# One hybrid attention layer on one core: the kernel lists the steps of TensorE, ScalarE and VectorE itself, adds Strassen products up in PSUM, and keeps high and low parts in one tile

## Chip, cores and metric

The kernel runs on one core of one Trainium2 chip. The metric is the device time of one execution in microseconds (us), lower is better. The core's engines are TensorE (PE, matmuls; its weight loads are shown apart as PEld), VectorE (DVE), ScalarE (ACT), GpSimd (POOL) and SyncE (SP, which here only issues transfers). Matmuls write into PSUM banks of 128 x 512 float32; everything else lies in SBUF tiles with 128 partitions.

## The reference, cut to what matters

One layer, batch 1, 512 tokens, model width 2048, three branches of four heads with 128 columns each.

```
hn   = rmsnorm(x, norm_g)                       # 512 x 2048
proj = hn @ w_in                                # 2048 x (6144 + 4 + 6144)
# the first 6144 columns: q, k, v and a gate path for branches A, B, C
# then 4 forget-gate logits, then 3 x 2048 merge-gate logits
ya = forgetting_attention(rms(q), rms(k), v, f_logit)      # A: softmax, causal
yb = chunked_relpos_attention(rms(q), rms(k), v, rel_bias) # B: softmax, 576-key band
yc = stick_breaking_attention(q, k, v)                     # C: products of 1 - sigmoid
ys = stack(ya, yb, yc) * silu(gate paths)
up = ys[n] @ w_up[n]                            # for each branch: 512 x 512 by 512 x 2048
merged = sum_n sigmoid(gate_n + b_gate) * up_n
out = x + merged @ w_out                        # 2048 x 2048
```

All inputs and outputs are float32.

## The kernel before

**Numbers and tiles.** Everything is kept transposed: model columns on partitions, the 512 tokens along a row. A product of float32 is made of three matmuls in the type fp32r: each operand is split into a high part (a copy rounded to fp32r) and a low part (the rest), and `mm3` (L115 to L118) adds up high x high, high x low and low x high. For a split, ScalarE writes the high part and VectorE the low part:

```python
def split_to(hi, lo, src):                              # L93
    nc.scalar.activation(hi, src, AF.Copy)              # L94
    nc.vector.tensor_sub(lo, src, f(hi))                # L95
```

In the program's names `wh` and `wl` are the parts of a weight piece, `x1h`, `x1l`, `x2h`, `x2l` those of the two halves of the normalized input (eight tiles of 128 x 512 each), `yh`, `yl` those of a branch's output, `m1`, `m2` those of the merged result. `split_off` (L104, so L106 and L107 in the profile) does the same with the low part put off by some splits.

**Units.** The program is a list of units; a unit has one weight piece of eight 128 x 128 blocks (128 x 1024; in the up-projections six blocks, 128 x 768), its load, its split, its matmuls, and what follows them. The stages in order:

- 0 to 64 us: the first head of branch C with its q, k, v and gate columns together (`first_quad`, L652), while x arrives and its norm is worked out.
- up to 117 us: four columns of merge gates, straight (`col_task`, L320, 512 columns of tokens a matmul).
- up to about 1100 us: the rest of the input projection in pairs of columns by a Strassen–Winograd scheme (`pair_task`, L334): two columns by two halves of the tokens in seven products P1 to P7 of 24 matmuls of 256 columns, in place of eight. Products 1, 2, 3 and 5 take x1 and x2; P6, P7 take `t23`, P4 takes `t`, sums of them made once in `combos` (L282). The weights' sums are made on VectorE for each pair (L351 to L363). A head uses two pairs (q and k, then v and gate) with pairs of merge gates between; their attention work lies beside later pairs. Merge gates go to HBM (`gl`), branch outputs too (`yd`).
- up to about 1235 us: the up-projections (`up_units`, L778): two units for each of 16 tiles of the model width, 12 tiles of y in each tile's sum; sigmoid (L806) on the gates that come back from HBM, products and sums on VectorE (L808 to L811), then the sums for the last Strassen stage (`merged_combos`, L826).
- to the end: the output projection, eight pairs, each with the residual added (L877 on).

**Banks and sums of a pair.** Each of the seven products takes the next of four PSUM banks `acc`, and its result is taken out by itself. A regular pair runs its products in the order 1, 2, 6, 7, 4, 5, 3; `u`, `c1` and `c2` are SBUF tiles, and one ScalarE copy and seven VectorE sums (L383 to L404) put the two columns together. The first pair, and the first of the output projection, run in the order 1, 2, 5, 3, 6, 7, 4 (`late=True`), in which what P6, P7 and P4 need may come later.

**What sets the order.** PE runs its instructions in the order in which the loop over the units (L962 on) writes them. Attention steps are hung on units by the table `OFF`. ScalarE and VectorE are in written order only up to unit 16 (`OFF["bgn"]`); from there on the framework's scheduler picks their order by its own model. A unit's split is written two units ahead (`LA`), its load five more (`LD`). Buffers: 21 tiles of 128 x 512 (`t2`), 56 for x, t, y and m parts, six for loaded weights.

## Time and profile before

| | before |
|---|---|
| median of 3 runs | 1401.34 us (1400.13 to 1402.62) |
| profiled execution | 1402.7 us, its span 1401.0 us |
| loads of w_in, w_up and w_out | 192 x 512, 32 x 384, 32 x 512 KB; 3.6, 3.1 and 3.8 us from issue to landing |
| moved by DMA | 180.57 MB, 129 GB/s over the span |
| share of 16 DMA engines, main queue | 39.3% |
| VectorE, splits of 128 x 1024 weights (L95) | 364 in 445.1 us |
| ScalarE, the same splits (L94) | 364 in 385.8 us |

The span is the time from the first to the last instruction of the profiled execution; the 1.7 us around it belong to its time. Busy time is the time in which an engine worked on something; waiting isn't in it. Matmuls overlap in the array, so a matmul's own duration (about 0.28 us for 256 columns) is longer than the distance from one start to the next. "Granted clock" is the share of TensorE's full clock that it was given. In rows of single instructions the columns are start (us), duration (us), engine, line, operation, output <- inputs, shape; x2 or more at the end is a group of such instructions, and a bracket tells how long the engine had waited and for whom.

### The profile page before, as it was taken

To read this page: it belongs to the slowest core of one execution; us is meant where nothing else is said; L and a number is where in the kernel's file an instruction comes from. 1 tells how busy PE (TensorE), PEld (TensorE's weight loads), DVE (VectorE), ACT (ScalarE), POOL (GpSimd) and SP (SyncE) were. 2 spreads that over 40 slices of the span, in tenths; PEclk is the share of its full clock that TensorE was granted. 3 is DMA by queue.
4 is the path that set the end of the run, shared out by engine and by line. 5 is a ranking of instruction groups with operands and counts; after the bars stand their busy time and mean duration, and the time that the engine had idled before them with its cause. 6 is when DMAs were issued, how large, how long until landed. Compare 5 with 4: busy or idle time off the path is not lost.

```text
span 1401.0 us, 25194 instructions
## 1 busy us (share of the span) xinstructions
PE 1370.5 (98%) x10306; PEld 1315.3 (94%) x10306; DVE 1163.9 (83%) x1687; ACT 743.9 (53%) x1095; POOL 4.3 (0%) x21
## 2 busy tenths in 40 slices
PE   7999999999999999999999999999999799999999
PEld 5778899999999999999999999999999688889999
DVE  4898898988879888898888878878888588898886
ACT  6655555544555555455556545555456655453332
POOL 0000000000000000000000000000000000000000
PEclk9999999999999999999999999999999899999999
DMA  9333233243333433333333333333335466535542
GB/s 338 129 107 101 90 95 115 99 128 106 100 123 111 128 104 120 124 102 125 116 112 121 95 126 119 99 121 93 128 104 174 164 202 206 170 95 172 166 148 80
DMA packets 68468, 180.57 MB, mean 129 GB/s; under 512 B 7656, under 2 KB 13672, under 8 KB 68352
## 3 DMA queue, kind: packets, MB, share of 16 engines
q1 hardware_dynamic: 64896, 174.69, 39.3%
q10 hardware_dynamic: 3456, 4.26, 0.9%
q8 instruction: 81, 1.33, 0.4%
q14 instruction: 35, 0.29, 0.1%
HBM read 159.24 MB, written 19.69 MB: 128 GB/s over the span
## 4 chain that ended last, share of the span: by engine, by line
PE 93%; DVE 3%; ACT 2%; DMA 1%; issue 1%; SPq 0%; ACTq 0%; DVEq 0%
PE acc L116 27%; PE acc L118 27%; PE acc L117 27%; PE att L117 3%; PE att L116 3%; PE att L118 3%; PE att L577 1%; DMA sg<-gl 1%; DVE wl L95 1%; PE att L546 1%; PE att L599 1%; PE att L431 1%; PE att L600 0%; PE att L598 0%; DMA x<-in_xT 0%
## 5 line engine op out<-in xcount | busy, mean ns | idle before, releaser
L94 ACT ACTIVATE wh<-raw 128x1024 fp32r<-128x1024 f32 x364 | 385.8, 1060 | 507.2 <-PE acc L117 455.4
L95 DVE TENSOR_TENSOR wl<-raw,wh 128x1024 fp32r<-128x1024 f32 x364 | 445.1, 1223 | 90.0 <-ACT wh L94 89.2
L116 PE MATMUL acc<-x1h,wh 128*128 128x256 f32 (+1 forms) x752 | 221.9, 295 | 12.9 <-ACT wh L106 9.6
L117 PE MATMUL acc<-x1l,wh 128*128 128x256 f32 (+1 forms) x752 | 219.3, 292 | 2.1 <-DVE x1l L107 2.1
L116 PE MATMUL acc<-x2h,wh 128*128 128x256 f32 (+1 forms) x752 | 220.9, 294 | 0.0
L118 PE MATMUL acc<-x1h,wl 128*128 128x256 f32 (+1 forms) x752 | 219.4, 292 | 1.1 <-DVE wl L107 1.0
L118 PE MATMUL acc<-x2h,wl 128*128 128x256 f32 (+1 forms) x752 | 218.5, 291 | 0.0
L117 PE MATMUL acc<-x2l,wh 128*128 128x256 f32 (+1 forms) x752 | 218.4, 290 | 0.0
L116 PE MATMUL acc<-t23h,wh 128*128 128x256 f32 x704 | 200.6, 285 | 0.0
L118 PE MATMUL acc<-t23h,wl 128*128 128x256 f32 x704 | 199.2, 283 | 0.0
L117 PE MATMUL acc<-t23l,wh 128*128 128x256 f32 x704 | 199.1, 283 | 0.0
L116 PEld LDWEIGHTS acc<-x1h,wh 128*128 128x128 f32 x752 | 144.9, 193 | 16.4 <-ACT wh L106 9.6
L117 PEld LDWEIGHTS acc<-x1l,wh 128*128 128x128 f32 x752 | 144.9, 193 | 4.9 <-DVE x1l L107 2.5
L118 PEld LDWEIGHTS acc<-x1h,wl 128*128 128x128 f32 x752 | 144.9, 193 | 4.2 <-DVE wl L107 2.3
L116 PEld LDWEIGHTS acc<-x2h,wh 128*128 128x128 f32 x752 | 144.8, 193 | 3.0 <-issue 0.2
L117 PEld LDWEIGHTS acc<-x2l,wh 128*128 128x128 f32 x752 | 144.7, 192 | 2.3 <-issue 0.2
L118 PEld LDWEIGHTS acc<-x2h,wl 128*128 128x128 f32 x752 | 144.5, 192 | 2.3 <-DVE wl L107 0.4
L117 PEld LDWEIGHTS acc<-t23l,wh 128*128 128x128 f32 x704 | 135.0, 192 | 0.0
L116 PEld LDWEIGHTS acc<-t23h,wh 128*128 128x128 f32 x704 | 135.0, 192 | 0.0
L118 PEld LDWEIGHTS acc<-t23h,wl 128*128 128x128 f32 x704 | 134.9, 192 | 0.0
L116 PE MATMUL acc<-t,wh 128*128 128x256 f32 x352 | 100.4, 285 | 0.0
L117 PE MATMUL acc<-t,wh 128*128 128x256 f32 x352 | 99.5, 283 | 0.0
(277 smaller groups left out, 2834.9 us busy)
## 6 DMA issues: line engine op xcount, KB each, us to landing
raw<-in_w_col SPq DMA_DIRECT2D x192, 512.0 KB, 3.6
raw<-in_w_out SPq DMA_DIRECT2D x32, 512.0 KB, 3.8
gl<-c SPq DMA_DIRECT2D x48, 256.0 KB, 2.0
raw<-in_w_up SPq DMA_DIRECT2D x32, 384.0 KB, 3.1
sg<-gl SPq DMA_DIRECT2D x48, 256.0 KB, 4.6
x<-in_xT SPq DMA_DIRECT2D x16, 256.0 KB, 6.2
xn<-in_xn SPq DMA_DIRECT2D x16, 256.0 KB, 6.2
xr<-in_xT SPq DMA_DIRECT2D x16, 256.0 KB, 4.8
```

Source lines behind the costliest of these rows:

```text
L94: nc.scalar.activation(hi, src, AF.Copy)
L95: nc.vector.tensor_sub(lo, src, f(hi))
L116: nc.tensor.matmul(ps, lh, rh, start=start, stop=False)
L117: nc.tensor.matmul(ps, lh, rl, start=False, stop=False)
L118: nc.tensor.matmul(ps, ll, rh, start=False, stop=stop)
L431: nc.tensor.matmul(first_ps[:2 * NH, :], w2[:, kt, :], xs[kt][j], start=kt + j == 0, stop=kt + j == KT)
L546: nc.tensor.transpose(ps[:, blk(i)], st["p"][i][:, blk(j)], identf)
L577: nc.tensor.matmul(ps[:, i * P:], nu_r if i == j else nones_r, part, start=i == j and part is st["lk"][j][0], stop=False)
L599: nc.tensor.matmul(o, vl[:, blk(j)], st["h"][j], start=False, stop=False)
```

## The change

The change has three parts.

**1. The order is made by the kernel.** All of PE, ScalarE and VectorE is now under `manual_schedule`, so that these three engines run what the program writes, in the order in which it writes it. Each step (a split, a softmax stage, the matmuls of one k-tile) is a generator that yields what it waits for (an `Event`, a number of `Slots` of a pool) and then `(engine, cost, due)` ahead of each instruction. `Flow.run` keeps a clock for each engine and always writes next the step that could start first, and of several the one that is due first. Costs are formulas, not measured times.

```diff
+class Flow:
+    LATE = (0.3, 0.12, 0.12)
...
+    def run(self):
+        while self.tasks:
...
+                    key = (max(self.clock[t.engine], t.ready), t.due)
+                    if best is None or key < best[0]:
+                        best = key, t
...
+            self.clock[e] = start + t.cost
+            t.ready = self.clock[e]
+            self.fin = t.fin = self.clock[e] + self.LATE[e]
...
+def mm_us(n, x=1):
+    return x * max(0.115, n / 2400 + 0.0133)
...
+def act_us(n, x=1):
+    return x * (0.075 + 0.00095 * n)
...
+def dve_us(n, x=1):
+    return x * (0.1 + 0.00105 * n)
...
-    ctx.enter_context(tc.manual_schedule(engines={mybir.EngineType.PE}))
-    begin = ExitStack()
-    begin.enter_context(tc.manual_schedule(engines={mybir.EngineType.Activation, mybir.EngineType.DVE}))
+    ctx.enter_context(tc.manual_schedule(engines={mybir.EngineType.PE, mybir.EngineType.Activation,
+                                                  mybir.EngineType.DVE}))
...
-OFF = dict(cs=4, ct=12, nk=5, nq=4, s=12, t=18, v=3, av=10, nrm=7, xg=10, bgn=16, fb=30, a0=16, b0=23, last=3)
+KEPT = 1
+NX = 28
+NR = 6
+
+OFF = dict(cs=3, ct=12, s=11, t=17, v=1, av=8, s1=8, t1=13, v1=0, av1=3, fb=30, a0=17, b0=27)
```

**2. Products of a pair add up in PSUM.** In a regular pair the order is now 1, 2, 6, 5, 7, 3, 4. P6 goes on in the bank of P1, P7 in that of P6, P4 in that of P7 (`onto`), P3 in that of P5; P2 has a bank of its own. The pool `acc` is now three: two banks of the first kind and one each of the others. ScalarE copies the sum so far out of a bank after P1, P6 and P5 (and after P4 where no residual is to be added), and VectorE adds after P2, P7 and P3. The matmuls are the same ones; the signs of some sums (`t4`, w6, w7) are turned for it. The first pair and the first output pair are as before in this, in the order 1, 5, 2, 3, 6, 7, 4. The last output pair is like the others now: the residual is added at P3, P7 and P4.

```diff
-        order = (1, 2, 5, 3, 6, 7, 4) if late else (1, 2, 6, 7, 4, 5, 3)
+            self.order = (1, 5, 2, 3, 6, 7, 4) if late else (1, 2, 6, 5, 7, 3, 4)
...
+            bank = (0, 1, 2, 0, 0, 1, 2)[i] if self.late else {2: 1, 5: 2, 3: 2}.get(p, 0)
+            onto = None if self.late else {6: 1, 7: 6, 4: 7, 3: 5}.get(p)
+            more = onto is not None
...
+                if more:
+                    yield self.ev[onto]
+                    self.ps[p] = self.ps[onto]
...
-                elif p == 7:
-                    add(u[:, RH], u[:, LH], ps)
...
-                elif p == 5:
-                    add(c2[:, RH], u[:, RH], ps)
-                    add(u[:, LH], u[:, LH], ps)
...
+                    if p == 6:
+                        yield a
+                        nc.scalar.activation(self.u[:, RH], ps, AF.Copy)
+                    elif p == 7:
+                        yield ev[5]
+                        yield v
+                        add(self.c2[:, RH], self.c2[:, RH], ps)
+                        finished("c2r", self.c2[:, RH])
```

**3. High and low parts lie in one tile.** `Parts` is a tile of 128 x 2 x 2 x 256: for each half of the tokens the high part, then the low part. A matmul over all 512 tokens reads its moving operand through `two(...)`, two runs of 256 with 256 others between. 28 such tiles stand for the 56 of before.

```diff
-    def xt(s):
-        return xp.tile([P, S], F32R, tag="x", name=nm(s))
...
+            self.t = xp.tile([P, 2, 2, HS], F32R, tag="x", name=nm(s))
+            self.hi, self.lo = self.t[:, :, 0, :], self.t[:, :, 1, :]
```

**Around the up-projections.** The sigmoid of a gate may be written only after the SiLU of the last head. A split of y is written four to one units ahead of the first up-projection. Of the sums for the last stage, those that need only the first half of the merged result (`merged_a`: m1) are made as soon as it is there; `merged_b` makes m2, then the differences, and, once the last up-projection's matmuls are written (`up_done`), the splits of m23 and m4 with due times of 7 and 14 us after it.

```diff
+            yield last_head.event("g")
+            yield ACT, act_us(S) + 0.1
+            nc.scalar.activation(g, g, AF.Sigmoid, bias=bg[:, n * DT + d:n * DT + d + 1])
...
+        yield up_done
+        yield xps, 1
+        due = up_done.t + 0.3 * k
+        ev = Event()
+        m23[k] = Parts("m23", [ev, ev])
+        yield from split(m23[k].hi, m23[k].lo, two(t), S, ev, (due + 7.0,))
```

**What stands in the rows of the engines.** ScalarE at the start of the up-projections, before (`y_13144` is the last head's SiLU, `sg` a merge gate, `yh` the high part of a branch's output, `wh` that of an up-projection's weights):

```order
L604 ACT_TABLE_LOAD
L604 ACTIVATE y_13144<-y_13144 128x512
L94 ACTIVATE yh_13053<-yr_13051 128x512
L605 ACT_TABLE_LOAD
L605 ACTIVATE y_13144<-y_13144 128x512
L106 ACTIVATE wh_13160<-raw_12955 128x768
L94 ACTIVATE yh_13095<-yr_13093 128x512
L806 ACT_TABLE_LOAD
L806 ACTIVATE sg_13099<-sg_13099,small_in 128x512
L607 ACT_TABLE_LOAD
L607 ACTIVATE y_13144<-y_13144 128x512
L806 ACT_TABLE_LOAD
```

The same place now (the split of y is a row of L239, with both halves in one instruction):

```order
L239 ACTIVATE y_12733<-yr_12664 128x2x256
L239 ACTIVATE y_12774<-yr_12666 128x2x256
L239 ACTIVATE y_12771<-y_12516 128x2x256
L239 ACTIVATE y_12718<-yr_12716 128x2x256
L239 ACTIVATE wh_12813<-raw_12556 128x768
L239 ACTIVATE y_12721<-yr_12719 128x2x256
L239 ACTIVATE y_12724<-yr_12722 128x2x256
L1316 ACT_TABLE_LOAD
L1316 ACTIVATE sg_12725<-sg_12725,small_in 128x512
L709 ACTIVATE c_12715<-acc_12519 128x256
L239 ACTIVATE wh_12849<-raw_12605 128x768
L239 ACTIVATE y_12767<-yr_12765 128x2x256
```

The steps of the last SiLU (L604 to L607) are no longer here but earlier, and the sigmoids begin after one table load.

VectorE at the start of the output projection, before (`m` the merged result, `m2l` and `m1l` the low parts of its last tile, `m23l` those of the sums for P6 and P7, `mt` and `mu` the sums themselves, `wl` a weight's low part):

```order
L811 TENSOR_TENSOR m_2349_14277<-m_2349_14277,sg_2330_14163 128x512
L830 TENSOR_TENSOR mt_2352_14290<-m_2349_14277,m_2340_14216 128x256
L831 TENSOR_TENSOR m_2340_14216<-m_2340_14216 128x256
L95 TENSOR_TENSOR m2l_2351_14287<-m_2349_14277,m2h_2350_14286 128x512
L832 TENSOR_TENSOR mt_2352_14290<-m_2349_14277,m_2340_14216 128x256
L95 TENSOR_TENSOR m1l_2354_14296<-m_2340_14216,m1h_2353_14295 128x512
L833 TENSOR_TENSOR mu_2327_14154<-mt_2352_14290,m_2349_14277 128x256
L95 TENSOR_TENSOR m23l_2356_14300<-mt_2230_13713,m23h_2355_14299 128x512
```

The same place now, from behind the last sum of the merged result (its tile is `sg_2068`) and one weight split; L625 is a sum of weights:

```order
L241 TENSOR_TENSOR m1_2096_13975<-sg_2056_13750,m1_2096_13975 128x2x256
L625 TENSOR_TENSOR raw_2073_13838<-raw_2073_13838,raw_2053_13732 128x1024
L241 TENSOR_TENSOR m23_2100_13982<-mt_1913_13017,m23_2100_13982 128x2x256
L241 TENSOR_TENSOR m23_2101_13983<-mt_1941_13160,m23_2101_13983 128x2x256
L241 TENSOR_TENSOR m23_2102_13984<-mt_1968_13301,m23_2102_13984 128x2x256
L241 TENSOR_TENSOR m23_2103_13985<-mt_1996_13443,m23_2103_13985 128x2x256
L241 TENSOR_TENSOR m23_2104_13986<-mt_2023_13584,m23_2104_13986 128x2x256
L241 TENSOR_TENSOR wl_2113_14035<-raw_2073_13838,wh_2112_14034 128x1024
L241 TENSOR_TENSOR m23_2105_13987<-mt_2051_13726,m23_2105_13987 128x2x256
L241 TENSOR_TENSOR m23_2106_13988<-mt_2078_13866,m23_2106_13988 128x2x256
L241 TENSOR_TENSOR wl_2119_14073<-raw_2053_13732,wh_2118_14072 128x1024
L241 TENSOR_TENSOR m2_2108_14023<-sg_2068_13818,m2_2108_14023 128x2x256
```

The last m1 now needs nothing of the last sum; the last m2, its split once directly behind the sum of the merged result, now stands behind seven of the eight m23 splits.

VectorE in the second regular pair (at 150 us of the profile before), before: `c_224` in the last row is the sum after that pair's P2, by which P2's bank comes free; `lk`, `lkl`, `z` belong to the first head's attention, L351 to L361 are sums of weights.

```order
L95 TENSOR_TENSOR lkl_1140<-lk_1329,lkh_1137 128x384
L351 TENSOR_TENSOR raw_1529<-raw_1393,raw_1395 128x1024
L565 SCALAR_TENSOR_TENSOR lk_1375<-z_1133,lk_1375 128x512
L95 TENSOR_TENSOR wl_1496<-raw_1105,wh_1495 128x1024
L360 TENSOR_TENSOR raw_1393<-raw_1391,raw_1393 128x1024
L566 TENSOR_TENSOR lk_1375<-lk_1375,m_104 128x128
L95 TENSOR_TENSOR wl_1526<-raw_1391,wh_1525 128x1024
L95 TENSOR_TENSOR lkl_1139<-lk_1375,lkh_1136 128x512
L385 TENSOR_TENSOR c_224_1367<-u_1366,acc_1399 128x256
```

The same pair now: L679 is the sum after P2, L1019 to L1026 are attention steps.

```order
L241 TENSOR_TENSOR wl_1329<-raw_1144,wh_1328 128x1024
L679 TENSOR_TENSOR c_1370<-c_1327,acc_1330 128x256
L1025 SCALAR_TENSOR_TENSOR lk_1262<-z_1169,lk_1262 128x384
L1026 TENSOR_TENSOR lk_1262<-lk_1262,m_104 128x128
L241 TENSOR_TENSOR lkl_1351<-lk_1220,lkh_1350 128x256
L241 TENSOR_TENSOR wl_1372<-raw_983,wh_1371 128x1024
L1025 SCALAR_TENSOR_TENSOR lk_1307<-z_1298,lk_1307 128x512
L1026 TENSOR_TENSOR lk_1307<-lk_1307,m_104 128x128
L241 TENSOR_TENSOR lkl_1260<-lk_1262,lkh_1259 128x384
L241 TENSOR_TENSOR wl_1408<-raw_1114,wh_1407 128x1024
```

The sum after P2 now stands ahead of the attention steps, which are spread between the weight splits; and its bank `acc_1330` is P2's alone, asked for again by the next pair.

## The prediction

> **What bounds it now.** I read the page first, then busy time by stage, then TensorE's own waits.

> ```profile
> span 1401.0 us, 25194 instructions
> PE 1370.5 (98%) x10306; PEld 1315.3 (94%) x10306; DVE 1163.9 (83%) x1687; ACT 743.9 (53%) x1095; POOL 4.3 (0%) x21
> ...
> PE 93%; DVE 3%; ACT 2%; DMA 1%; issue 1%; SPq 0%; ACTq 0%; DVEq 0%
> ```

> TensorE (PE) is busy for 98% of the span and holds 93% of the chain that ended last. A busy PE is not always a PE at full pace, so the next view, busy time by stage, is read with its column PEclk (after the POOL column).

> ```profile
> 65.00:122.00 57.00, 53.90 (x268) 45.49 (x267) 52.69 (x111) 28.81 (x54) 0.00 (x0) 0.99 0.32 99
> 150.00:160.00 10.00, 6.68 (x42) 6.42 (x40) 7.65 (x13) 3.12 (x4) 0.00 (x0) 0.83 0.19 54
> 160.00:1080.00 920.00, 920.00 (x7565) 913.70 (x7564) 782.87 (x1093) 500.77 (x727) 1.51 (x3) 1.00 0.36 113
> 1080.00:1112.00 32.00, 24.12 (x123) 19.63 (x122) 18.73 (x32) 24.92 (x35) 0.00 (x0) 0.84 0.60 213
> 1112.00:1232.00 120.00, 120.00 (x534) 99.48 (x533) 97.99 (x150) 61.25 (x86) 0.00 (x0) 1.00 0.54 177
> 1232.00:1242.00 10.00, 6.69 (x44) 6.29 (x43) 9.93 (x17) 6.54 (x14) 0.00 (x0) 0.83 0.21 57
> ```

> From 160 to 1080 us PE is busy for 920.00 of 920.00 us at full clock, from 1112 to 1232 for 120.00 of 120.00. Nothing can be won there. The time above PE's own work lies in four places: 65 to 122 (norm, and first Strassen pair), 150 to 160 (second regular pair), 1080 to 1112 (start of the up-projections), 1232 to 1242 (start of the output projection). PE's waits by releaser give the sizes; the columns after the colon are us in total, times, longest.

> ```profile
> PE acc L116 <- ACT wh L106: 9.6, 1, 9.6
> PE att L116 <- ACT yh L94: 7.1, 2, 5.3
> PE acc L116 <- DVE c L385: 3.3, 1, 3.3
> PE acc L116 <- ACT m1h L94: 2.8, 1, 2.8
> PE acc L117 <- DVE x1l L107: 2.1, 2, 1.5
> PE acc L118 <- DVE wl L107: 1.0, 1, 1.0
> PE att L117 <- DVE yl L95: 0.8, 2, 0.6
> PE acc L117 <- DVE m1l L95: 0.5, 1, 0.5
> ```

> The 9.6 us are the first load and split. The other 17.6 us have a second price, which the clock column shows after three of the waits and at the up-projections:

> ```profile
> 121.00:124.40 3.40, 3.40 (x16) 3.40 (x17) 1.71 (x2) 1.33 (x2) 0.00 (x0) 0.51 0.37 136
> 1101.00:1111.00 10.00, 5.63 (x13) 4.19 (x14) 4.84 (x7) 6.96 (x10) 0.00 (x0) 0.51 0.03 10
> ```

> After the two L117 waits the granted clock is 0.51 for 3.4 us: half of that, 1.7 us, is lost. In the ten microseconds to 1111 PE ran 5.63 us at 0.51: 2.8 us lost. The stage rows 150 to 160 and 1232 to 1242, at 0.83 over 10 us, give 1.7 us each. So PE's removable loss is 17.6 + 1.7 + 2.8 + 1.7 + 1.7 = 25.5 us of 1401.0.

> **PE's own work.** The order of instructions has the same matmuls before and now: 8836 of 256 columns, 1077 of 512, 32 of 8 x 512, 92 of 384, 268 of 128. Their pace is the distance of starts:

> ```profile
> 70.42 0.39 PE L116 MATMUL acc<-x1h,wh 128*128 128x512 f32 x1
> 70.65 0.39 PE L117 MATMUL acc<-x1l,wh 128*128 128x512 f32 x1
> ...
> 150.70 0.28 PE L117 MATMUL acc<-t,wh 128*128 128x256 f32 x1
> 150.82 0.28 PE L118 MATMUL acc<-t,wl 128*128 128x256 f32 x1
> 154.42 0.35 PE L116 MATMUL acc<-x1h,wh 128*128 128x256 f32 x1 [3.31 <-DVE c L385]
> ```

> 0.23 us for 512 columns, 0.12 for 256; a Strassen product of 24 matmuls takes 2.88 us. The change removes no PE work. It can only remove waits, and add some.

> **Removed: the wait at 150 (3.3 + 1.7 = 5.0 us).** Before, each of a pair's seven products takes a new one of four banks, so the sixth product, P5, waits for P2's bank, whose sum (L385) stood on VectorE behind a weight split, two source sums and an attention split. Now P1, P6, P7, P4 add up in one bank, P5 and P3 in another, P2 has a third: P2's bank is not asked for again before the next pair's P2, seven products or 20 us later. I count 5.0 us gone.

> **Removed: the waits from 65 to 122 (1.0 + 2.1 + 1.7 = 4.8 us).** At 70.65 (third row up) PE stood for the second column task's wl, which VectorE made after the first head's evacuations; now that split stands ahead of them. At 118 to 121 it stood for the last x1 difference. VectorE rows from the evacuations (64.4 us, end of the first head's columns) to the last combination are now 12 of 1024 elements, 11 of 512, 64 of 256. Spacings come from VectorE's and ScalarE's timeline:

> ```profile
> 1237.83 1.89 DVE L95 TENSOR_TENSOR m23l<-mt,m23h 128x512 fp32r<-128x512 f32 x3
> 1239.68 1.23 DVE L95 TENSOR_TENSOR wl<-raw,wh 128x1024 fp32r<-128x1024 f32 x1
> 1240.82 1.29 DVE L95 TENSOR_TENSOR m23l<-mt,m23h 128x512 fp32r<-128x512 f32 x2
> 1242.03 1.76 DVE L95 TENSOR_TENSOR m<-mu,m 128x256 fp32r<-128x256 f32 x5
> 1243.70 0.42 DVE L385 TENSOR_TENSOR c<-u,acc 128x256 f32<-128x256 f32 x1
> ...
> 1236.61 1.65 ACT L94 ACTIVATE m23h<-mt 128x512 fp32r<-128x512 f32 x3
> 1238.59 1.06 ACT L94 ACTIVATE wh<-raw 128x1024 fp32r<-128x1024 f32 x1 [0.33 <-PE acc L118]
> 1239.55 0.37 ACT L383 ACTIVATE u<-acc 128x256 f32<-128x256 f32 x1
> ```

> Start to start, VectorE needs 1.14 us for 1024, 0.60 for 512, 0.33 for 256 (up to 0.46 where one reads the other's result); ScalarE 0.96, 0.55 and about 0.3. So 12 x 1.14 + 11 x 0.60 + 64 x 0.33 to 0.46 = 41 to 50 us: done by 106 to 114. PE comes to t23 at 64.4 + 192 x 0.227 + 4 x 2.88 = 119.5, and the differences for P5 stand earlier still. The forget-gate's some twenty small instructions, which lay among them (L443 to L456), now follow later. 4.8 us gone.

> **Removed: the up-projections' start (7.1 + 0.8 + 2.8 = 10.7 us).** ScalarE changed its table between sigmoid and the SiLU's exp and ln:

> ```profile
> 1100.23 1.28 ACT L607 ACT_TABLE_LOAD   x1
> 1101.53 0.63 ACT L607 ACTIVATE y<-y 128x512 f32<-128x512 f32 x1
> 1102.17 1.28 ACT L806 ACT_TABLE_LOAD   x1
> 1103.47 1.33 ACT L806 ACTIVATE sg<-sg,small_in 128x512 f32<-128x512 f32 x2
> 1104.71 0.61 ACT L94 ACTIVATE yh<-y 128x512 fp32r<-128x512 f32 x1
> ```

> The last yh, for which PE stood longest, came behind five such loads. Now no sigmoid comes before the last SiLU is done (one load), and that SiLU and the last a·v stand three products before the first up-projection. Twelve y splits must fit: they can start when x1's tiles are free, three products (8.6 us) ahead of the first up-projection. VectorE then has 12 x 0.60 + 3 weight splits + 2 sums, some 11 us, and PE asks for y10, the last in the order, 8.6 + 10 x 0.68 = 15.4 us after that point. By the same rows, with ScalarE's waits for weight buffers, y10 is done at about 15.6. I keep 0.2 us and count 10.5 gone.

> **Moved: the output projection's start.** Before it cost 2.8 + 0.5 + 1.7 = 5.0 us. m1 is now made during the up-projections, but VectorE's new row there (in the change, above) puts seven m23 splits ahead of the last m2. From PE's last up-projection VectorE has, in order: product and sum 1.20, wl 1.14, m1[7] 0.60; a source sum 1.14, five m23 3.0, wl 1.14, two m23 1.2, wl 1.14, m2[7] 0.60. With 0.16 us until a matmul's result is there (0.28 busy less 0.12 pace) m1[7] is ready at 3.1 and m2[7] at 11.3 us. PE asks for m1[7] at 22 x 0.12 = 2.6 and for m2[7] at 5.76 + 2.64 = 8.4: waits of 2.9 us together. Then m23[7] stands behind P4's wl, whose wh waits for P3's end: 0.16 + 0.96 + 1.14 + 0.33 + 0.55 + 0.60 = 3.7 us after it, asked for at 2.64: 1.1 us more. Idle 4.0 us, and one stretch of half clock as after the waits above, 1.7: 5.7 us, that is 0.7 more than before.

> [...]

> **Added, at nothing.** Fifty regular pairs now have three sums on VectorE in place of seven and four copies on ScalarE in place of one: 200 x 0.33 off, 150 x 0.3 on. In the 920-us stage ScalarE is busy for 500.77 and VectorE for 782.87, so both hide. New for PE: P6 may not start before ScalarE has copied P1 (cover: P2's 2.88 us), P7 before P6's copy, P3 before P5's, P4 before P7's sum, each with one product of cover. A copy that finds a weight split (1.06) just begun needs 0.16 + 1.06 + 0.37 = 1.6 us: hidden. Bounds from rows: nothing, to one such split late in each pair, 50 x 1.06 = 53 us; I take nothing, since two splits and more must stand ahead. It cannot be a gain, PE has no idle time there. In the 512-column matmuls the moving operand is now two runs of 256, with the low part between. Bounds: nothing, to the pace of two matmuls of 256, 1077 x (0.24 - 0.227) = 14 us; no gain, since the same columns pass. I take nothing: 256-column matmuls already read half of a 512-wide tile at 0.12. The first 65 us and the end (one sum, one 128-KB store after the last product) keep their chains; I count 0.

> **Sum.** -5.0 - 4.8 - 10.5 + 0.7 = -19.6 us. The profiled execution took 1402.7 (span 1401.0), which gives 1383.1; the runs' median is 1401.34, 1.4 lower, and on it the forecast is 1381.7, rounded **1382 us**.

> **Rivals.** *The output start is smooth as well* (5.7 us less, 1376). For it: the m23 splits' due times in the plan are later than the weight splits'. Against: the row's order is fixed. *Small waits in the pairs*: the hand order is made with fixed costs and each engine runs it in order; a tenth to a third of a us in 50 pairs gives 5 to 16 us, 1388 to 1398. Against: its costs (0.12 for a matmul of 256, 1.175 and 1.05 for splits) are at or above the rows here. *Two-run operand*: 14 us, 1396. [...] *Nothing gained*: the weight splits come later by what the waits were, 1398.5 to 1404.1. Against: VectorE has 17% idle and loses 66 us of sums. *Slower*: ScalarE's copy of P1 comes more than 2.88 us after P1, because splits and softmax steps stand ahead in its queue, and PE stands in each pair; from 0.45 us a pair (22.4 us over 50 pairs) the kernel is over 1404.1, with a whole split of 1.06 it is 1435. For it: before, a sum came 3.3 us late once in 52 pairs. Against: ScalarE's 54%.

> **Chances.** Forecast (1377 to 1388) 0.58; smooth output start 0.10; small waits 0.15; two-run operand 0.03; nothing gained 0.05; slower 0.09. A measurement of this kernel can tell about 0.2%, 2.8 us, from no change: faster 0.86, same 0.05, slower 0.09. The range 1373 to 1397 holds the first three and most of the fourth, and leaves out some 0.17.

> **What will show it.** Right: PE busy for all of 65 to 122 and 150 to 160; one table load of 1.28 us near 1080 and PE waits for y under 1 us; PE waiting 3 to 4 us for m1, m2 and m23 at about 1215. Wrong: a line among PE's waits on ScalarE's copies (L673, L689, L683) or on L693 with a count near 50; 512-column matmuls starting more than 0.23 us apart; more than one stretch of half clock after 130 us, which would mean that I misread an order as smooth.

## The result and the profile after

| | before | after |
|---|---|---|
| median, range (4 runs each) | 1401.98 us, 1400.13 to 1403.06 | 1381.94 us, 1380.36 to 1382.54 |
| ratio, 95% interval | | 0.9857, 0.984 to 0.9874 |
| span of the profiled execution | 1401.0 us | 1380.8 us |

20 us less, forecast 1382. The engines' busy time, from the page of the changed kernel:

```profile
PE 1363.8 (99%) x10306; PEld 1311.4 (95%) x10306; DVE 1100.3 (80%) x1488; ACT 772.3 (56%) x1233; POOL 4.4 (0%) x21
```

TensorE (PE) has the same 10306 matmuls. VectorE (DVE) works 64 us less, ScalarE (ACT) 28 us more. Busy time by stage, with the columns of before (the granted clock stands after POOL):

```profile
65.00:122.00 57.00, 57.00 (x307) 49.54 (x306) 50.39 (x94) 28.55 (x56) 0.00 (x0) 1.00 0.32 98
150.00:160.00 10.00, 10.00 (x87) 10.00 (x86) 9.55 (x23) 6.56 (x14) 0.00 (x0) 1.00 0.17 56
160.00:1080.00 920.00, 920.00 (x7553) 913.23 (x7552) 731.62 (x938) 537.54 (x861) 1.57 (x3) 1.00 0.38 118
1068.00:1100.00 32.00, 32.00 (x183) 28.18 (x182) 26.04 (x41) 24.07 (x39) 0.00 (x0) 1.00 0.76 276
1210.00:1225.00 15.00, 12.18 (x87) 11.77 (x86) 14.10 (x23) 9.70 (x20) 0.00 (x0) 0.89 0.26 78
```

In three of the four places PE is now busy throughout at full clock; the start of the output projection (1210 to 1225) is what is left. PE's waits of the whole execution (us in total, times, longest):

```profile
PE acc L247 <- ACT wh L239: 9.1, 1, 9.1
PE acc L248 <- DVE m L241: 3.2, 3, 2.2
PE acc L247 <- ACT m L239: 0.8, 1, 0.8
PE acc L249 <- DVE wl L241: 0.7, 1, 0.7
```

The first is the first load, as before. The other 4.7 us stand in the output projection, seen in TensorE's own timeline:

```profile
1212.12 0.39 PE L248 MATMUL acc<-m,wh 128*128 128x256 f32 x1 [0.62 <-DVE m L241]
...
1220.34 0.47 PE L248 MATMUL acc<-m,wh 128*128 128x256 f32 x1 [2.21 <-DVE m L241]
...
1228.50 0.38 PE L247 MATMUL acc<-m,wh 128*128 128x256 f32 x1 [0.77 <-ACT m L239]
1229.22 0.38 PE L248 MATMUL acc<-m,wh 128*128 128x256 f32 x1 [0.34 <-DVE m L241]
...
1242.18 0.39 PE L249 MATMUL acc<-m,wl 128*128 128x256 f32 x1 [0.70 <-DVE wl L241]
```

These are m1[7] (0.62; forecast 0.5), m2[7] (2.21; 2.4) and m23[7] (0.77 + 0.34; 1.1). Behind the second, 3.4 us at 0.52 of the clock cost 1.6 us (forecast 1.7):

```profile
1220.35:1223.75 3.40, 3.40 (x16) 3.40 (x17) 3.40 (x9) 1.06 (x1) 0.00 (x0) 0.52 0.57 154
```

The 0.70 us at 1242, a low weight of the second output pair, were not forecast.

### The profile page after: what moved, and what is told of

It reads as the page before. It is cut to its first block, busy times and chain, and to the rows that moved or that the text cites. A ratio compares the mean times of both kernels' runs of the same rounds, so it can differ in the third digit from the quotient of the medians.

```text
span 1380.8 us, 25041 instructions
## 1 busy us (share of the span) xinstructions
PE 1363.8 (99%) x10306; PEld 1311.4 (95%) x10306; DVE 1100.3 (80%) x1488; ACT 772.3 (56%) x1233; POOL 4.4 (0%) x21
## 3 DMA queue, kind: packets, MB, share of 16 engines
q8 instruction: 81, 1.33, 0.4%
## 4 chain that ended last, share of the span: by engine, by line
PE 97%; DVE 2%; DMA 1%; issue 0%; ACT 0%; SPq 0%
PE acc L247 28%; PE acc L249 27%; PE acc L248 27%; PE att L248 3%; PE att L249 3%; PE att L247 3%; PE att L1042 1%; PE att L971 1%; DVE wl L241 1%; PE att L754 1%; PE att L1109 1%; PE att L1110 1%; PE att L1108 1%; DMA x<-in_xT 0%; PE att L1069 0%
## 5 line engine op out<-in xcount | busy, mean ns | idle before, releaser
L241 DVE TENSOR_TENSOR wl<-raw,wh 128x1024 fp32r<-128x1024 f32 (+1 forms) x412 | 493.7, 1200 | 192.1 <-ACT wh L239 191.0
L239 ACT ACTIVATE wh<-raw 128x1024 fp32r<-128x1024 f32 (+1 forms) x412 | 428.3, 1040 | 307.8 <-PE acc L248 201.1
L247 PE MATMUL acc<-x,wh 128*128 128x256 f32 (+1 forms) x1504 | 440.4, 293 | 9.1 <-ACT wh L239 9.1
L249 PE MATMUL acc<-x,wl 128*128 128x256 f32 (+1 forms) x1504 | 436.4, 290 | 0.1
L248 PE MATMUL acc<-x,wh 128*128 128x256 f32 (+1 forms) x1504 | 436.1, 290 | 0.0
L247 PEld LDWEIGHTS acc<-x,wh 128*128 128x128 f32 x1504 | 288.3, 192 | 15.4 <-ACT wh L239 9.1
L247 PE MATMUL acc<-t,wh 128*128 128x256 f32 x1056 | 301.2, 285 | 0.0
L249 PE MATMUL acc<-t,wl 128*128 128x256 f32 x1056 | 298.7, 283 | 0.0
L248 PE MATMUL acc<-t,wh 128*128 128x256 f32 x1056 | 298.7, 283 | 0.0
L248 PEld LDWEIGHTS acc<-x,wh 128*128 128x128 f32 x1504 | 288.2, 192 | 4.8 <-DVE wl L241 0.2
L249 PEld LDWEIGHTS acc<-x,wl 128*128 128x128 f32 x1504 | 287.9, 191 | 4.7 <-DVE wl L241 0.8
L247 PEld LDWEIGHTS acc<-t,wh 128*128 128x128 f32 x1056 | 202.4, 192 | 0.5
L248 PEld LDWEIGHTS acc<-t,wh 128*128 128x128 f32 x1056 | 202.4, 192 | 0.5
L248 PE MATMUL acc<-m,wh 128*128 128x256 f32 x448 | 127.8, 285 | 3.2 <-DVE m L241 3.2
L247 PE MATMUL acc<-m,wh 128*128 128x256 f32 x448 | 127.5, 285 | 0.8 <-ACT m L239 0.8
L625 DVE TENSOR_TENSOR raw<-raw,raw 128x1024 f32<-128x1024 f32 x52 | 63.4, 1220 | 0.6
```

Of the source, the lines that this page charges most:

```text
L247: nc.tensor.matmul(ps, lh, rh, start=start, stop=False, skip_group_check=more)
L248: nc.tensor.matmul(ps, lh, rl, start=False, stop=False, skip_group_check=more)
L249: nc.tensor.matmul(ps, ll, rh, start=False, stop=stop, skip_group_check=more)
L625: nc.vector.tensor_sub(w[3], w[2], w[6])
```

## The experiments

Twelve kernels, in three groups: parts of the change undone or done alone, the margin of the new waits, and the start of the output projection. Comparisons are with the medians above; kernels made from the kernel before are compared with its 1400.25 us in the same group of runs. The kernel before was run again beside each group (1401.68, 1401.90 and 1400.25 us), the changed kernel was not, so a difference of one or two us from its 1381.94 isn't read as one.

### One part undone

**The accumulation in PSUM, first way**: every pair runs as the first one does.

```diff
+            late = True
             self.ops, self.late, self.rest = ops, late, rest
```

> The changed kernel with the accumulation in PSUM undone: every pair runs like the first one (order 1, 5, 2, 3, 6, 7, 4, each product in a bank by itself, two ScalarE copies and seven VectorE sums). Theory of the prediction (the wait of 5.0 us at 150 went because the banks are no longer asked for early): it comes back, and with 200 sums of 0.33 more on VectorE it may come in other pairs too: 1387 or more. Rival (the listed order alone removed it, and the sums lie beside PE's work): 1381 to 1383, no PE wait between 120 and 1080 us.

Measured: 1392.60 us (1392.13 to 1393.22), 10.7 more. Nothing at 150, but seven waits of 1.4 us between 428 and 963 us. This also moves P5 to the second place, whose weight is a sum that must be made first, so the next kernel separates the two.

**The accumulation, second way**: regular pairs with the products' order, banks and sums of before, in the listed order of the changed kernel.

```diff
-            self.order = (1, 5, 2, 3, 6, 7, 4) if late else (1, 2, 6, 5, 7, 3, 4)
+            self.order = (1, 5, 2, 3, 6, 7, 4) if late else (1, 2, 6, 7, 4, 5, 3)
...
+            bank = (0, 1, 2, 0, 0, 1, 2)[i]
+            onto = None
```

> The changed kernel with the pairs of before: order 1, 2, 6, 7, 4, 5, 3, each product in a bank by itself, one ScalarE copy and seven VectorE sums; the first pairs of both stages as they are. Unlike the run with own banks, P5 stands late. Theory A (the seven waits of that run for P5's and its neighbours' low weights came from the order of its products): no PE wait from 120 to 1080 us, 1381 to 1384. Theory B (200 sums more on VectorE are what makes splits late): waits of 1 to 2 us in some pairs again, 1387 to 1395. Prediction's step (early banks bring the wait at 150 back): 5 us at 150, 1387.

Measured: 1389.74 us (1389.29 to 1390.18), 7.8 more (9.5 by the ratios to the kernel before in each group). PE's waits between 120 and 1080 us, and the stage from 160:

```profile
PE acc L249 <- DVE wl L241: 5.6, 8, 0.7
```

```profile
160.00:1080.00 920.00, 914.37 (x7495) 906.31 (x7495) 784.94 (x1100) 498.40 (x723) 1.51 (x3) 1.00 0.36 115
```

Theory B, with waits of 0.7 us in place of 1 to 2. Against the changed kernel's row VectorE has 53 us more in this stage, and in eight pairs, in which a head's norm (L891) stands beside the weight sums, a low weight comes 0.7 us late. With what each wait costs besides, by estimate (a matmul's 0.28 us less its pace of 0.12, 0.16 us), these are 8 x 0.86 = 6.9 us. Two more things differ between the profiled executions, whose spans are 6.7 us apart: the end behind the last matmul is 1.1 us longer here, and the half clock at the output projection, 1.6 us in the changed kernel, is absent. There is no wait at 150: the changed program without the accumulation removes that one too.

**The accumulation alone, in the kernel before**: order 1, 2, 6, 5, 7, 3, 4, three banks to a pair, the signs turned; all else as before.

```diff
+                onto = None if late else {6: 1, 7: 6, 4: 7, 3: 5}.get(p)
+                more = onto is not None
+                st["ps"] = st["ps", p] = ps = st["ps", onto] if more else acc()[:, LH]
```

> The kernel before with only the accumulation in PSUM: order 1, 2, 6, 5, 7, 3, 4, three banks to a pair, four ScalarE copies and three VectorE sums; ScalarE and VectorE as the framework orders them. Theory of the prediction (this alone takes the wait at 150 away): 5 us less than before, 1396 to 1397. Rival (what stands in ScalarE's and VectorE's rows decides, and four copies must now come in time in a row that nobody times): PE waits for copies in pairs, 1402 or more.

Measured: 1436.96 us (1435.60 to 1437.35), 36.7 more than before, ratio 1.026 (1.0243 to 1.0278). PE's longest group of waits is new, and ScalarE's timeline ahead of one of them shows how it comes about:

```profile
PE acc L116 <- ACT u L386: 29.5, 13, 5.2
```

```profile
259.68 1.06 ACT L94 ACTIVATE wh<-raw 128x1024 fp32r<-128x1024 f32 x1 [1.03 <-PE acc L117]
260.64 1.02 ACT L576 ACTIVATE lk<-lk 128x384 f32<-128x384 f32 x2
261.57 1.03 ACT L577 ACTIVATE lk<-lk 128x384 f32<-128x384 f32 x2
263.56 1.04 ACT L94 ACTIVATE lkh<-lk 128x384 fp32r<-128x384 f32 x2 [0.96 <-DVE lk L579]
264.50 0.37 ACT L386 ACTIVATE u<-acc 128x256 f32<-128x256 f32 x1
```

```profile
264.92 0.58 PE L116 MATMUL acc<-t23h,wh 128*128 128x256 f32 x1 [5.17 <-ACT u L386]
```

The copy of P1 (L386) stands in ScalarE's row behind a weight split, the stick-breaking attention's exp and ln, and two splits, of which one waits for VectorE; PE, which may not add P6 to that bank before, stands for 5.17 us. This is the mechanism of the rival "slower", in 13 of the 50 pairs; half clock behind some of these waits adds to it (granted 0.985 over the span, before 0.994). The wait of 3.3 us for VectorE at 150 is gone here too, but in the same pair, at 141.7 us, PE stands 1.3 us for the copy.

**ScalarE's and VectorE's listed order**: only TensorE stays under `manual_schedule`, the program is the same.

```diff
-    ctx.enter_context(tc.manual_schedule(engines={mybir.EngineType.PE, mybir.EngineType.Activation,
-                                                  mybir.EngineType.DVE}))
+    ctx.enter_context(tc.manual_schedule(engines={mybir.EngineType.PE}))
```

> The changed kernel with only TensorE's order listed; ScalarE's and VectorE's are picked by the framework's scheduler from the same program. Theory (the order of ScalarE and VectorE carries the gains at 65 to 122 us and at the start of the up-projections, 4.8 and 10.5 us): most of these come back, 1392 or more. Rival (the accumulation in PSUM and the place of the steps in the program carry the gain): within 3 us of 1382.

Measured: 1387.98 us (1387.30 to 1388.62), 6.0 more, but not where the theory had it. All of TensorE's waits, and two stages:

```profile
PE acc L247 <- ACT x L239: 16.5, 1, 16.5
PE acc L249 <- DVE wl L241: 3.2, 3, 2.5
PE acc L247 <- ACT wh L239: 1.2, 1, 1.2
```

```profile
72.00:130.00 58.00, 58.00 (x318) 50.61 (x317) 48.03 (x100) 28.18 (x57) 0.00 (x0) 1.00 0.36 107
1080.00:1110.00 30.00, 30.00 (x155) 25.73 (x155) 22.75 (x36) 20.28 (x31) 0.00 (x0) 1.00 0.75 262
```

The first matmul starts at 16.5 us instead of 9.1, because the framework puts squares of x ahead of the first split of x. No wait came back at 72 to 130 or at the up-projections, and none of TensorE's waits is for a ScalarE copy out of PSUM. So it isn't the held order of ScalarE and VectorE that carries those two gains, but what else the change did: above all the order in which the steps now stand in the program (and on PE). Which of the moved steps did it from 65 to 122 us was not tried one by one.

**The tile of high and low parts**: the 512 high values together.

```diff
-            self.hi, self.lo = self.t[:, :, 0, :], self.t[:, :, 1, :]
+            self.hi, self.lo = self.t[:, 0, :, :], self.t[:, 1, :, :]
```

> The changed kernel with the 512 high values of a tile side by side, then the 512 low ones, so that a 512-column matmul reads one run instead of two of 256. Theory (two runs cost nothing, starts 0.227 us apart either way): 1381 to 1383. Rival (the two-run operand costs up to 0.013 us in 1077 matmuls): up to 14 us less, 1368.

Measured: 1379.92 us (1379.41 to 1382.03), 2.0 less, with ranges that overlap, and no 14 us. Most of the two us is the clock's: three of these four executions have a granted clock of 1.000 (1379.41 to 1380.00 us) and one 0.999 (1382.03), while of the changed kernel's one has 1.000 (1380.36 us) and three 0.999 (1381.84 to 1382.54). At the same clock at most 1 us is left. The pace settles it. Two rows of the changed kernel, with the two-run operand:

```profile
1204.63 0.39 PE L247 MATMUL att<-y,wh 128*128 128x512 f32 x1
1204.86 0.39 PE L248 MATMUL att<-y,wh 128*128 128x512 f32 x1
```

0.23 us from start to start, as before and as in this run (1204.19 and 1204.42 us).

### The start of the up-projections

**The SiLU late again**: the last head's SiLU and a·v at the first up-projection.

```diff
+            if self.last:
+                return g, [(v, self.v_trans), (7, self.silu), (7, self.av)]
```

> The changed kernel with the last head's SiLU and a.v put at the first up-projection, where the kernel before has them; sigmoids still come after that SiLU, so there is one table load. Theory (the place of the SiLU decides when the last y is ready): four ScalarE steps, three VectorE steps and a split are about 6 us, with weight and y splits between some 11 us, and PE asks for the last y after 7.5: waits of 3 to 4 us and 1.7 of half clock, 1385 to 1388. Rival (only the table loads made it late before): no wait, 1382.

Measured: 1382.22 us (1381.73 to 1382.70), no change that can be told. PE's waits for y:

```profile
PE att L247 <- ACT y L239: 0.5, 1, 0.5
PE att L248 <- DVE y L241: 0.2, 1, 0.2
```

The place alone costs 0.7 us of waits, not the 3 to 4 that were expected.

**The same, and the sigmoids free to come before it**:

```diff
-            yield last_head.event("g")
             yield ACT, act_us(S) + 0.1
```

> As the run with the late SiLU, but sigmoids may also come before it: four table loads in place of one. Theory (each table load of 1.28 us ahead of the last y's split delays it): 3 x 1.28 us and one sigmoid of 0.7 more than the run with the late SiLU alone, some 4 to 5 us, 1390 to 1393. Rival (the loads are hidden beside VectorE's steps): the same as that run.

Measured: 1390.64 us (1390.08 to 1390.91), 8.4 more than the run with the late SiLU. PE's waits from 1070 to 1110 us, and two of the four table loads, which now stand between the SiLU's steps:

```profile
PE att L247 <- ACT y L239: 4.7, 1, 4.7
PE att L248 <- DVE y L241: 0.9, 2, 0.5
```

```profile
1079.93 1.28 ACT L1088 ACT_TABLE_LOAD   x1
...
1082.91 1.28 ACT L1092 ACT_TABLE_LOAD   x1
```

4.9 us more of waits, as the theory had it, and half clock behind them (0.50 from 1090.0 to 1093.4 us), which the expectation left out. The late SiLU with sigmoids held back (the run above) and the early SiLU without that (the next run, in the kernel before) both have one table load here and hardly a wait; what both do is to keep table loads out from between the SiLU's steps. The changed kernel without the `yield` alone was not run.

**The SiLU early, alone, in the kernel before**: its six steps as a stage by itself, eight units earlier.

```diff
+        if last:
+            at(u0 + 20, st["silu"])
```

> The kernel before with one edit: the last head's SiLU is written eight units earlier, ahead of the sigmoids; ScalarE's row then has one table load near the up-projections in place of six. Theory (the table loads made the last y late): the waits of 7.1 and 0.8 us for y and most of the half clock there go, 8 to 10.5 us less than before, 1391 to 1394. Rival (they were hidden, and y was late because its splits were written late): within 2 us of 1401.5.

Measured: 1388.67 us (1387.98 to 1390.32), 11.6 less than before, ratio 0.992 (0.9905 to 0.9934). Its waits for y:

```profile
PE att L116 <- ACT yh L94: 0.3, 1, 0.3
PE att L117 <- DVE yl L95: 0.2, 1, 0.2
```

Of 7.9 us for y 0.5 is left, and one table load stands near the up-projections in place of six. This one move, of six instructions, brings more than half of what the whole change brings.

### The margin of the new waits

**ScalarE's copy of P1 six times, and eleven times, in every regular pair** (the same values; the listed order is unchanged):

```diff
                 if p == 1:
                     yield a
+                    for _ in range(0 if self.late else 5):    # 10 in the second kernel
+                        nc.scalar.activation(self.u[:, LH], ps, AF.Copy)
```

> The changed kernel with ScalarE's copy of P1 made six times over in each of the 50 regular pairs (the same values): 5 x 0.3 = 1.5 us more. Theory (P6 waits for the copy, P2's 2.88 us cover it): done 0.16 + 1.5 + 0.37 = 2.0 us after P1, hidden but where a split of 1.06 stands ahead (ScalarE came late in 20 of 52): 0 to 5 us, 1382 to 1387. Rival (the cover is smaller than a product, because splits always stand ahead): 0.5 us and more in each pair, over 1407.

Measured: 1398.42 us (1397.48 to 1399.94, 10 runs), 16.5 more, three times what was expected at most. In the list of PE's waits the copy stands once, with 0.2 us. The split of the squares on ScalarE at a head's second norm, first in the changed kernel, then with the copies ahead of it:

```profile
404.19 0.63 ACT L239 ACTIVATE sqh<-sq 128x512 fp32r<-128x512 f32 x1
```

```profile
402.38 2.05 ACT L674 ACTIVATE c<-acc 128x256 f32<-128x256 f32 x5 [0.37 <-PE acc L249]
...
406.34 0.63 ACT L239 ACTIVATE sqh<-sq 128x512 fp32r<-128x512 f32 x1
```

```profile
407.02 0.49 PE L871 MATMUL att<-sqh,ones_r 128*128 128x512 f32 x1 [0.63 <-ACT sqh L239]
```

The split of the squares, which stands behind the copies, a weight split and the square itself, came 2.1 us later, and PE's matmul for the norm stood for it. Eight of sixteen norms did this, 7.0 us of waits for the two parts, and 16 times the 0.16 us of the estimate above: 9.6 us. Other late splits add 2.7 us of waits. The copy's own cover held in most pairs, not in all: at 427.69 us and six places like it P6 starts 0.28 us late behind the last copy, which hides in the end of the matmul before and so isn't counted as a wait; these are some 2 us. The rest was not traced.

> As before with the copy made eleven times over: 3.0 us more. Theory: done 3.5 us after P1 and more, 0.6 to 1.7 us over P2's cover in each of 50 pairs: 30 to 85 us more, 1412 to 1467, with PE waiting on the line of that copy some 50 times. Rival (P6 does not wait for the copy, or ScalarE's row runs ahead far enough): within 5 us of 1382.

Measured: 1501.41 us (1498.38 to 1503.70), 119.5 more, far over the expected 85. PE's longest group of waits:

```profile
PE acc L247 <- ACT c L675: 63.9, 39, 2.1
```

The wait for the copy is there and within its bounds (64 us in 39 pairs). What the expectation missed is again what it sets off: the norms (10.8 us of waits), the 0.16 us of the estimate beside each wait, and half clock; the granted clock is 0.981 over the span, up to 28 us of 1499.

### The start of the output projection

**m2 first**: the m23 splits wait until the last m2 is split.

```diff
+        if k == UK - 1:
+            set_(m2_done)
...
         yield up_done
+        yield m2_done
```

> The changed kernel, but the m23 splits wait until the last m2 is split. Theory (TensorE's waits at the start of the output projection come from VectorE's row, where seven m23 splits stand ahead of m2[7], and one half-clock window follows the longest): the 2.2 us for m2[7], the 0.8 and 0.4 for m23[7] and 1.7 us of half clock go, the 0.6 for m1[7] stays: 5 us less than the changed kernel, about 1377. Rival (the work in that row is too much for the time, so that the wait only moves to m23 or m4): no change, about 1382, with TensorE waits of 3 to 4 us at P6 or P4.

Measured: 1381.58 us (1380.21 to 1382.05), no change. The waits for m2[7] and m23[7] are gone, and 2.1 us for a low weight of the second output pair at 1238 with half clock behind it (0.50 from 1238.5 to 1241.9 us) stand in their place, so the rival held, with another place than it named.

**m2 first, m1 without slack, the first pair's residual sums 7 us later**:

```diff
-                    spawn(merged_a(d, m[0]), 5.0, flow.fin)
+                    spawn(merged_a(d, m[0]), 0.0, flow.fin)
...
-                    spawn(self.done[name](c), 1.0, flow.fin)
+                    spawn(self.done[name](c), 8.0 if self.late else 1.0, flow.fin)
```

> The changed kernel with m2 ahead of the m23 splits, m1's steps without slack, and the first output pair's residual sums due 7 us later. Theory (VectorE's row is full from 1209 to 1237, and moving what nobody waits for behind the low weights of the second pair takes the wait of 2.1 us at 1236 away): PE idles under 1.5 us there, no half clock, 1376 to 1379. Rival (the row has too much work for the time, whatever the order): a wait of 1 to 2 us elsewhere in it, 1380 to 1382.

Measured: 1380.68 us (1380.00 to 1381.48), 1.3 less, with ranges that overlap: not shown to be faster (its ratio to the kernel before in its own group is 0.9861, the changed kernel's 0.9857). Its waits from 1209 to 1245 us, its busy time there, and the half clock behind the last of them:

```profile
PE acc L249 <- DVE wl L241: 3.2, 2, 1.7
PE acc L247 <- ACT wh L239: 0.8, 1, 0.8
```

```profile
1209.00:1237.00 28.00, 25.23 (x206) 24.61 (x205) 27.90 (x44) 17.23 (x29) 0.00 (x0) 1.00 0.29 99
1238.30:1241.70 3.40, 3.40 (x17) 3.40 (x18) 1.67 (x3) 0.00 (x0) 0.00 (x0) 0.54 0.76 187
```

VectorE is busy for 27.90 of 28 us, and PE still waits 4.0 us in all, with half clock behind: the rival. In both orders that were tried VectorE bounds this stretch, and the order only moves the wait. Work would have to leave VectorE here; that was not tried.

## Why the prediction was right, point by point

- **The bound.** Right: PE's own work is the same, and the change took the waits off it. The sum of the terms came out at -19.6, the spans differ by 20.2; this close a sum is in part luck, since the small misses have both signs (the first load, counted at 0, was 0.5 us shorter; the others stand below).
- **65 to 122 us, -4.8.** Right in size: PE is busy for 57.00 of 57.00 us at full clock. The cause as given (where the low parts stand in VectorE's row) fits the trace but was not isolated; the run without the held order shows that holding VectorE's order isn't needed. The stop that the text puts at 70.65 us ends at 72.08.
- **150 us, -5.0.** Right in size, wrong in the cause. "Now P1, P6, P7, P4 add up in one bank": the bank is sufficient for this wait (the accumulation alone removes it in the kernel before, and brings waits for the copies) but not needed (the changed program with the old banks has no wait there either).
- **Up-projections, -10.5.** Right: 10.7 removed, and the one move made alone in the kernel before brings 11.6. Of the two reasons given, table loads and the earlier SiLU, the table loads decide: the late SiLU without them costs 0.7 us of waits, with them 5.6.
- **Output projection, +0.7.** It came to +1.3: each of the three waits is right to 0.2 us and the half clock to 0.1, and 0.7 us for the second pair's low weight were missed. The half clock was partly luck. With the same wait of 2.2 us for m2[7] the clock stayed full in the runs with the late SiLU and with the old pairs (1.000 over the span in both); what decides it was not shown.
- **"Added, at nothing".** Right for the changed kernel (no PE wait from 160 to 1080 us, pace 0.23). But "both hide" named the wrong cover: the 200 VectorE sums hide beside PE only in part; put back, they cost 7.8 us. In the kernel before, in the order that the framework had found, they were free (PE busy for 920.00 of 920.00 us).
- **The rivals.** Slower was given 0.09, from copies of P1 behind softmax steps. It is real: the same accumulation in the program of before is 36.7 us slower by such waits and the half clock behind them. What kept it off is the place of each copy in ScalarE's row, not ScalarE's 54%, which the prediction held against it. That place doesn't need the hand order: with the framework's order of the changed program no such wait came. The two-run operand costs nothing that can be told. Small waits in the pairs did not come, and the output start was not smooth.

The gains don't add up: the early SiLU alone is worth 11.6 us, the accumulation alone -36.7, the accumulation within the changed program some 8, and all together 20.

## What to carry to other kernels

When PE is busy for 98%, list its waits with what stands ahead of the releaser in that engine's row; an ACT_TABLE_LOAD there (1.28 us each here) is the first thing to move, and moving six instructions can bring more than half of what a rewritten schedule brings (here 11.6 of 20 us). Adding products up in PSUM trades work on VectorE for copies with a short deadline: the same step cost 36.7 us in one program and was worth some 8 in the other, by where each copy stands in its row, and an engine's share of busy time (54%) doesn't tell that. The margin of such a deadline is not the cover of the one wait but of everything that stands behind it in the same row.

## What the runs showed of the hardware

Whether a stall cost clock as well was not decided by its length alone. In the run with eleven copies two stalls of the same length ended differently. First the waits in TensorE's timeline:

```profile
137.78 0.38 PE L247 MATMUL acc<-t,wh 128*128 128x256 f32 x1 [1.75 <-ACT c L675]
```

```profile
264.85 0.39 PE L247 MATMUL acc<-t,wh 128*128 128x256 f32 x1 [1.76 <-ACT c L675]
```

Then, behind each, 3.40 us with PE's busy time and, behind POOL, the granted clock:

```profile
137.80:141.20 3.40, 3.40 (x18) 3.40 (x19) 2.46 (x5) 3.37 (x6) 0.00 (x0) 0.58 0.11 12
264.90:268.30 3.40, 3.40 (x28) 3.40 (x29) 2.49 (x5) 2.51 (x5) 0.00 (x0) 1.00 0.13 17
```

The first was followed by half clock, the second was not. In the kernel before, half clock was granted four times behind the start:

```profile
120.90:124.31 3.41, 3.41 (x16) 3.41 (x17) 1.62 (x2) 1.33 (x2) 0.00 (x0) 0.50 0.38 137
155.03:158.44 3.41, 3.41 (x18) 3.41 (x18) 2.15 (x5) 0.00 (x0) 0.00 (x0) 0.50 0.02 5
1100.52:1110.76 10.24, 5.39 (x12) 3.99 (x13) 4.84 (x7) 7.44 (x10) 0.00 (x0) 0.50 0.06 23
1237.05:1240.46 3.41, 2.91 (x14) 2.83 (x14) 3.41 (x6) 3.08 (x7) 0.00 (x0) 0.50 0.16 65
```

In the changed kernel the 2.21 us for m2[7] were followed by half clock from 1220.49 to 1223.91 us, the waits of 0.62, of 0.77 and 0.34, and of 0.70 us were not. In the run with own banks the clock was 1.00 behind the wait of 1.41 us at 429.76. So a wait of 1.75 us and one of 2.21 us were followed by half clock, one of 1.76 us and, in the run with the late SiLU (granted clock 1.000 over the span), one of 2.2 us were not; what decides between them was not shown. Executions of one kernel differ in it too: of the changed kernel's four one has a granted clock of 1.000 and three 0.999.
